# Sixty-four bytes behind each split-weight buffer of a hybrid decoder layer

## The chip, the core and the metric

The kernel runs on one core of one Trainium2 chip. The metric is the device time of one execution, in microseconds (us). The kernel before takes 1090.24 us, the median of three runs (1089.42, 1090.24 and 1090.95 us). The profile shown below is of another, single execution of the same program, which took 1090.18 us; its span from the first to the last recorded instruction is 1088.3 us, so 1.9 us lie around the span.

## What is computed

One decoder layer for 256 tokens of width 2048, in float32. Cut to the matrix products, which is where nearly all the time is:

```python
h = rmsnorm(x, pre_mix_g)
proj = h @ w_in                          # 2048 x 4368: q, k, v of two attention groups, forget gates
o_a = swa_sink_attention(...)            # 16 heads, window 128, sinks, ALiBi
o_b = forgetting_attention(...)          # 16 heads, learned forget gates
mix = concatenate([rmsnorm(o_a), rmsnorm(o_b)]) @ w_out      # 2048 x 2048
x = x + rmsnorm(mix, post_mix_g)
h = rmsnorm(x, pre_ffn_g)
u = causal_dwconv(h @ w_up, conv_w, conv_b)                  # 2048 x 11264
gate, val = split(u, 2)
y = (gelu(gate) * val) @ w_down                              # 5632 x 2048
x = x + rmsnorm(y, post_ffn_g)
```

All weights together are some 200 MB and each is used once, on 256 tokens.

## The kernel before

**Split operands.** Every float32 operand of a large product is kept as two tensors of the type float32r: a high part (the value as the copy to float32r leaves it) and a low part (the value less the high part). A product is then three matmuls: high by high, high by low and low by high.

**Weights.** `w_load` (L66) brings one unit of 128 x 1024 float32 (512 KB) by a DMA from SP's queue into one of five buffers named `raw`. `w_split` (L93) makes the two parts: ACT copies `raw` into a buffer `whi` (L103), and DVE subtracts `whi` from `raw` into a buffer `wlo` (L106). In one stage `w_high` (L81) does the same with L86 and L89. The buffers come from `w_parts` (L73). It has three cases: with `keep` unset, the ten ring buffers of the pool `wp`, five `whi` and five `wlo` (`WB = 5`, L64); with a pool in `keep`, buffers of that pool under the tags `hhi` and `hlo`; with `None` in `keep`, slices that the caller gives. The ring cases are nearly all: a `keep` with a pool is used for four units of the output projection, and the given slices for two units of the down projection. All these tensors are called `whi` and `wlo` in the profile, except the slices, which are called `rest`.

**Two ways in which PE reads the weights.** A matmul on this machine takes a stationary operand of 128 columns, which a weight load (PEld) brings in, and a moving operand that streams past it.

- In `unit_T` (L205) the weights are stationary. A unit has 8 slices of 128 columns (512 bytes in each partition) for each part. For each slice of `whi`, all 512 columns of `hT` (256 high, 256 low) stream past (L212); for each slice of `wlo`, the 256 high columns (L217). So a unit is 8 matmuls of 512 columns and 8 of 256. All of the q and k projections and the whole up projection go this way, the first four units of the up projection in a special form (L830, L834).
- In `mm3` (L241) the weights are moving. A stationary slice of 128 columns is taken from `hT` (the v projection), `oT` (the output projection) or `G` (the down projection), and a row of `whi` or `wlo` streams past it: L245, three matmuls for each pair, in the order `whi`, `wlo`, `whi`. The rows have 512 columns (2048 bytes) in the output and down projections. In the v projection they have 384 columns (1536 bytes), and in its last group 272 (1088 bytes). In that last group a unit holds three such rows one behind another, so they start 0, 1088 and 2176 bytes into the buffer, which is 0, 64 and 128 modulo 512. For each of the three rows, six matmuls follow one another.

**Order.** PE's instructions are in the order of the program (`manual_schedule`, L46). ACT, DVE, POOL and SP are placed by the framework's scheduler except in the stages where the program fixes them too.

**Addresses.** In SBUF each pool is laid out in the order `const`, `main`, `wp`, `small`, and then the pools of the stages. Three unused tiles named `room` (in `const`, `small` and `ffn`) shift what follows them. In the built program all large operands of PE start at a multiple of 512 bytes within a partition: `hT`, the five `raw`, the ten split buffers (from 106496 on, 4096 apart), `oT`, `G`, `keys`, `vpa` and `vpb`. Some tiles of the attention do not: `p`, `ph`, `pl`, `qh`, `ql` and `ident` start at 128 modulo 512.

- `L445` transposes a block of `p`: `p` is stationary at 128 modulo 512. `L681` transposes a block of `x_sb`: `x_sb` is stationary at 0. The moving operand of both is `ident`.
- `L454` and `L456` stream `ph` and `pl` (128 modulo 512, in two runs) past `vpa` or `vpb` (stationary, 0 modulo 512).

Of the kernel before, what the change touches and what calls it, by code (L numbers as in the profile page):

```python
# [8 lines left out]
F32 = mybir.dt.float32  # L9
F32R = mybir.dt.float32r  # L10
# [7 lines left out]
P = 128  # L18
# [12 lines left out]
def hybrid_layer(ctx: ExitStack, tc: tile.TileContext, x, pre_mix_g, w_in, b_forget, sinks,  # L31
# [10 lines left out]
    wp = ctx.enter_context(tc.tile_pool(name="wp", bufs=4))  # L42
    small = ctx.enter_context(tc.tile_pool(name="small", bufs=4))
# [19 lines left out]
    UNIT = 1024  # L63
    WB = 5  # L64
# [8 lines left out]
    def w_parts(n, keep=None):  # L73

        if keep and keep[0] is None:
            return keep[1]
        where, pre, nb = (keep[0], "h", keep[1]) if keep else (wp, "w", WB)
        return [where.tile([P, UNIT], F32R, tag=pre + x, bufs=nb, name="w" + x)[:, :n]
                for x in ("hi", "lo")]

    def w_high(unit, keep=None):  # L81

        raw, a, c = unit
        n = a * c
        hi, lo = w_parts(n, keep)
        act.copy(hi, raw[:, :n])  # L86

        def low():
            dve.tensor_tensor(lo, raw[:, :n], hi.bitcast(F32), op=ALU.subtract)  # L89

        return [x.rearrange("p (a c) -> p a c", a=a) for x in (hi, lo)], low

    def w_split(unit, pin=False, keep=None, begun=None, between=None):  # L93

        raw, a, c = unit
        n = a * c
        hi, lo = begun or w_parts(n, keep)
        for i in range(2 if between else 1):
            cs = slice(i * 512, i * 512 + 512) if between else slice(0, n)
            if i:  # L100
                between()
            if not between or i:
                i1 = act.copy(hi[:, cs], raw[:, cs])  # L103
                if pin:
                    tc.keep_in_program_order(i1)
            i2 = dve.tensor_tensor(lo[:, cs], raw[:, cs], hi[:, cs].bitcast(F32), op=ALU.subtract)  # L106
            if pin:
                tc.keep_in_program_order(i2)
        return [x.rearrange("p (a c) -> p a c", a=a) for x in (hi, lo)]

    def w_unit(src, a, c, keep=None):
        return w_split(w_load(src, a, c), keep=keep)

    def w_rows(w, k0, a, c0, c):
        return w[k0 * P:(k0 + a) * P, c0:c0 + c].rearrange("(a p) c -> p a c", p=P)
# [8 lines left out]


    const.tile([P, 120], F32, tag="room", name="room_c")
    small.tile([P, 368], F32, tag="room", bufs=1, name="room_s")

    gpre = const.tile([16, P], F32, tag="gpre", name="gpre")
    act.dma_start(gpre, pre_mix_g.rearrange("o (a p) -> (o a) p", p=P))  # L130
# [120 lines left out]
    with tc.tile_pool(name="mixp", bufs=1) as mp:  # L251
# [47 lines left out]


        begun = w_parts(UNIT)
        tc.keep_in_program_order(dve.tensor_copy(begun[0][:, 0:512], head[:, 0:512]))
        x_part(0, (0,), "acc")
# [246 lines left out]
        for p0, npair, cols in ((0, 3, 384), (3, 3, 384), (6, 2, 272)):  # L550
# [3 lines left out]
            for k0 in range(0, KT, per):  # L554
                na = min(per, KT - k0)
                hi, lo = w_unit(w_rows(w_in, k0, na, c0, cols), na, cols)
# [207 lines left out]
    with tc.tile_pool(name="ffn", bufs=1) as fp:  # L764
# [90 lines left out]
        for half in range(2):  # L855
# [42 lines left out]
            for n in range(3 + (half == 0)):  # L898
                b2 = [bank(), bank()]
                for u in range(FHALF // 2):  # L900
                    hi, lo = w_unit(w_rows(w_down, half * FHALF + u * 2, 2, n * 512, 512), 2, 512)
# [33 lines left out]
        for u in range(FHALF // 2):  # L935
            hi, lo = w_unit(w_rows(w_down, FHALF + u * 2, 2, 1536, 512), 2, 512,
                            keep=(None, [rest[:, c:c + 2, :].rearrange("p a c -> p (a c)")
                                         for c in (4 * (u - LAST), 4 * (u - LAST) + 2)])
                            if LAST <= u < FHALF // 2 - 4 else None)
# [56 lines left out]
```

## Time and profile before

| | |
|---|---|
| median of three runs | 1090.24 us |
| profiled execution, its own time | 1090.18 us |
| its span | 1088.3 us |
| mean granted TensorE clock | 0.996 |
| q, k, v projections and attention | 0 to 242 us |
| output projection, norms, residual | 242 to 342 us |
| up and down projection, first half | 342 to 713 us |
| up and down projection, second half | 713 to 1088 us |

In the profile an engine is busy while one of its instructions runs. Matmuls overlap: one that is listed with 389 ns starts some 227 ns after the one before. So the distance between the starts says what a matmul costs a full stream, and the listed length (which is longer by a nearly constant part) serves to compare matmuls of the same width. PEld is the weight load, which runs under the matmul before it. In the rows of the groups, the columns are: line, engine, operation, output <- inputs, shape and count | busy time in us, mean length of one in ns | idle time of the engine just before them, and what ended it. In the rows of a timeline, they are: start in us, length in us, engine, line, operation and count; neighbours of one kind are merged into a row.

### The profile page before, as it was taken

The page shows a single profiled execution, that of the slowest core. Times are in us where ns is not written, and L with a number is a line of the kernel's source. Part 1 is how long each engine was busy: PE and PEld are TensorE (multiplying, and loading weights), DVE is VectorE, ACT ScalarE, POOL GpSimd, SP SyncE. Part 2 cuts the span into 40 slices and gives each one's busy share as a digit, 9 for nine tenths or more (in the row PEclk, how much of TensorE's full clock was granted, in tenths as well). Part 3 has the DMA queues.
Part 4 walks back from the last instruction along what each step waited for, and adds up shares of the span by engine and source line. Part 5 has one row for each costly group of instructions (what it writes and reads, how often), then busy time and mean ns, then how long its engine had stood idle before and what let it go on. Part 6 is the DMA issues. An engine that isn't in the chain of part 4 may idle for free.

```text
span 1088.3 us, 16295 instructions
## 1 busy us (share of the span) xinstructions
PE 1075.0 (99%) x6002; PEld 932.2 (86%) x6002; DVE 739.7 (68%) x1193; ACT 625.7 (57%) x1069; POOL 183.3 (17%) x252
## 2 busy tenths in 40 slices
PE   9999999999999999999999999999999999999996
PEld 7889988887889888888888888888888888888886
DVE  5987877777567876776767544457777677765563
ACT  7766766666556765656656444456565565644450
POOL 3343344332022110101001000001010110101111
PEclk9999999999999999999999999999999999999998
DMA  8645565554872666656565666655665666666552
GB/s 291 196 129 170 174 190 177 153 158 152 284 243 104 213 197 193 191 178 198 186 193 183 199 192 194 197 189 180 189 195 182 192 191 186 184 196 192 193 171 78
DMA packets 164970, 202.88 MB, mean 186 GB/s; under 512 B 6780, under 2 KB 130972, under 8 KB 164380
## 3 DMA queue, kind: packets, MB, share of 16 engines
q1 hardware_dynamic: 164176, 201.27, 58.2%
q8 instruction: 47, 0.77, 0.3%
q10 hardware_dynamic: 716, 0.58, 0.2%
q14 instruction: 31, 0.25, 0.1%
HBM read 199.58 MB, written 2.11 MB: 185 GB/s over the span
## 4 chain that ended last, share of the span: by engine, by line
PE 89%; DVE 4%; ACT 3%; issue 1%; POOL 1%; DMA 1%; SPq 0%; DVEq 0%; POOLq 0%; ACTq 0%
PE bank_acc L245 34%; PE bank_acc L212 20%; PE bank_att L212 14%; PE bank_acc L217 10%; PE bank_att L217 7%; DVE wlo L106 2%; ACT whi L103 1%; POOL scr L377 1%; PE bank_att L410 1%; PE bank_att L454 1%; PE bank_att L445 1%; ACT p L428 1%; DMA x_in<-in_x_dram 1%; PE bank_att L456 0%; DVE hT L691 0%
## 5 line engine op out<-in xcount | busy, mean ns | idle before, releaser
L106 DVE TENSOR_TENSOR wlo<-raw,whi 128x1024 fp32r<-128x1024 f32 (+3 forms) x357 | 452.8, 1271 | 245.9 <-ACT whi L103 244.2
L103 ACT CAST whi<-raw 128x1024 fp32r<-128x1024 f32 (+3 forms) x356 | 368.5, 1037 | 235.9 <-PE bank_acc L245 119.0
L212 PE MATMUL bank_acc<-hT,whi 128*128 128x512 f32 x1120 | 286.7, 393 | 0.0
L212 PEld LDWEIGHTS bank_acc<-hT,whi 128*128 128x128 f32 x1120 | 200.0, 189 | 34.6
L245 PE MATMUL bank_acc<-whi,G 128*128 128x512 f32 (+1 forms) x724 | 214.8, 379 | 0.0
L212 PE MATMUL bank_att<-hT,whi 128*128 128x512 f32 x672 | 170.9, 392 | 0.1
L217 PEld LDWEIGHTS bank_acc<-hT,wlo 128*128 128x128 f32 x1120 | 151.3, 190 | 9.9
L217 PE MATMUL bank_acc<-hT,wlo 128*128 128x256 f32 x1120 | 157.6, 283 | 0.0
L245 PEld LDWEIGHTS bank_acc<-whi,G 128*128 128x128 f32 x724 | 133.8, 188 | 25.7 <-DVE y_sb L892 0.2
L801 POOL TENSOR_TENSOR u<-u,rowf 128x256 f32<-128x256 f32 x88 | 55.4, 651 | 543.3 <-DVE u L800 541.0
L212 PEld LDWEIGHTS bank_att<-hT,whi 128*128 128x128 f32 x672 | 120.7, 189 | 21.7 <-ACT whi L103 0.3
L245 PE MATMUL bank_acc<-wlo,G 128*128 128x512 f32 (+1 forms) x362 | 137.1, 379 | 0.0
L217 PEld LDWEIGHTS bank_att<-hT,wlo 128*128 128x128 f32 x672 | 91.7, 190 | 7.0 <-DVE wlo L106 0.4
L217 PE MATMUL bank_att<-hT,wlo 128*128 128x256 f32 x672 | 94.0, 282 | 0.0
L245 PE MATMUL bank_acc<-whi,oT 128*128 128x512 f32 (+1 forms) x272 | 83.1, 382 | 0.0
L245 PEld LDWEIGHTS bank_acc<-wlo,G 128*128 128x128 f32 x362 | 68.1, 188 | 12.8
L245 PEld LDWEIGHTS bank_acc<-whi,oT 128*128 128x128 f32 x272 | 50.4, 189 | 9.4
L245 PE MATMUL bank_acc<-wlo,oT 128*128 128x512 f32 (+1 forms) x136 | 51.5, 379 | 0.0
L245 PE MATMUL bank_acc<-whi,hT 128*128 128x384 f32 (+1 forms) x192 | 47.5, 323 | 0.0
L428 ACT ACTIVATE p<-p,nm 128x256 f32<-128x256 f32 (+1 forms) x64 | 28.4, 445 | 28.4 <-DVE nm L416 28.4
L377 POOL TENSOR_TENSOR scr<-scr 128x256 f32<-128x256 f32 x26 | 26.8, 1049 | 49.2 <-DVE scr L376 43.3
L799 ACT COPY cs<-bank_acc 128x256 f32<-128x256 f32 x48 | 15.9, 372 | 32.3 <-PE bank_acc L212 32.3
(187 smaller groups left out, 963.9 us busy)
## 6 DMA issues: line engine op xcount, KB each, us to landing
raw<-in_w_up_dram SPq DMA_DIRECT2D x176, 512.0 KB, 3.4
raw<-in_w_down_dram SPq DMA_DIRECT2D x88, 512.0 KB, 4.6
raw<-in_w_in_dram SPq DMA_DIRECT2D x51, 512.0 KB, 3.9
raw<-in_w_out_dram SPq DMA_DIRECT2D x32, 512.0 KB, 4.6
raw<-in_w_in_dram SPq DMA_DIRECT2D x16, 384.0 KB, 3.8
cb<-c_dram SPq DMA_DIRECT2D x8, 256.0 KB, 3.5
x_sb<-in_x_dram SPq DMA_DIRECT2D x2, 1024.0 KB
raw<-in_w_in_dram SPq DMA_DIRECT2D x5, 408.0 KB, 3.3
```

Source lines behind the costliest of these rows:

```text
L103: i1 = act.copy(hi[:, cs], raw[:, cs])
L106: i2 = dve.tensor_tensor(lo[:, cs], raw[:, cs], hi[:, cs].bitcast(F32), op=ALU.subtract)
L212: pe.matmul(b, hi[:, a, m * P:(m + 1) * P], hT[:, kt, :], start=(kt == 0), stop=(kt == KT - 1))
L217: pe.matmul(b[:, 256:512], lo[:, a, m * P:(m + 1) * P], hT[:, u * 4 + a, 0:256], start=False, stop=False)
L245: pe.matmul(b, a, r[:, cols], start=(first and i == 0), stop=(last and i == 2))
L377: pool.tensor_tensor(dst, dst, row, op=ALU.mult)
L410: pe.matmul(sb[e][:, cs], a[r, t * P:(t + 1) * P], b[r, 0:nk], start=(n == 0), stop=(n == 2))
L428: act.activation(p[:, e, cs], p[:, e, cs], AF.Exp, bias=nm[:, t, e:e + 1], scale=-1.0, accum_out=rs[:, t, e:e + 1])
L445: pe.transpose(pb[:, i * P:(i + 1) * P], p[:, e, c:c + P], ident)
L454: pe.matmul(ov, values(hl, 0), p[:, :, 0:256], start=(n == 0), stop=False)
L799: act.copy(c, b[:, 256:512])
L801: pool.tensor_tensor(u[:, 2:258], u[:, 2:258], rowf, op=ALU.mult)
```

## The change

`w_parts` gives the ring buffers of the pool `wp` 1040 columns in place of 1024 and goes on using the first 1024; the cases with `keep` are as before. The unused tile in `small` shrinks from 368 to 208 columns, by 640 bytes, which is ten times 64.

```diff
         if keep and keep[0] is None:
             return keep[1]
-        where, pre, nb = (keep[0], "h", keep[1]) if keep else (wp, "w", WB)
-        return [where.tile([P, UNIT], F32R, tag=pre + x, bufs=nb, name="w" + x)[:, :n]
+        if keep:
+            return [keep[0].tile([P, UNIT], F32R, tag="h" + x, bufs=keep[1], name="w" + x)[:, :n]
+                    for x in ("hi", "lo")]
+
+        return [wp.tile([P, UNIT + 16], F32R, tag="w" + x, bufs=WB, name="w" + x)[:, :n]
                 for x in ("hi", "lo")]
...
     const.tile([P, 120], F32, tag="room", name="room_c")
-    small.tile([P, 368], F32, tag="room", bufs=1, name="room_s")
+    small.tile([P, 208], F32, tag="room", bufs=1, name="room_s")
```

In the built program the five `whi` then start at 0, 64, 128, 192 and 256 modulo 512, and the five `wlo` at 320, 384, 448, 0 and 64. Every other tensor keeps its address. Each engine has the same instructions with the same shapes and waits in the same order; only the addresses of the ten buffers in them differ. All lines after the edited function move down by 3.

## The prediction

> **What bounds the kernel now.** I read the page first, then the groups with their shapes kept apart, then the chain of waits, and last a timeline of a stage in which the weights already lie off 512.
>
> ```profile
> span 1088.3 us, 16295 instructions
> ...
> PE 1075.0 (99%) x6002; PEld 932.2 (86%) x6002; DVE 739.7 (68%) x1193; ACT 625.7 (57%) x1069; POOL 183.3 (17%) x252
> ...
> PE 89%; DVE 4%; ACT 3%; issue 1%; POOL 1%; DMA 1%; SPq 0%; DVEq 0%; POOLq 0%; ACTq 0%
> PE bank_acc L245 34%; PE bank_acc L212 20%; PE bank_att L212 14%; PE bank_acc L217 10%; PE bank_att L217 7%; DVE wlo L106 2%; ACT whi L103 1%; POOL scr L377 1%; PE bank_att L410 1%; PE bank_att L454 1%; PE bank_att L445 1%; ACT p L428 1%; DMA x_in<-in_x_dram 1%; PE bank_att L456 0%; DVE hT L691 0%
> ```
>
> PE is busy for 99% of the span and makes 89% of the chain that ended last. The three lines that read the changed buffers, L245, L212 and L217, hold 34 + 20 + 14 + 10 + 7 = 85% of it. So the time moves with the distance between the starts of these matmuls, and with hardly anything else. The weight loads show the counts, and whether PE waits for the split:
>
> ```profile
> L212 PEld LDWEIGHTS bank_acc<-hT,whi 128*128 128x128 f32 x1120 | 200.0, 189 | 34.6
> L217 PEld LDWEIGHTS bank_acc<-hT,wlo 128*128 128x128 f32 x1120 | 151.3, 190 | 9.9
> L245 PEld LDWEIGHTS bank_acc<-whi,G 128*128 128x128 f32 x724 | 133.8, 188 | 25.7 <-DVE y_sb L892 0.2
> L212 PEld LDWEIGHTS bank_att<-hT,whi 128*128 128x128 f32 x672 | 120.7, 189 | 21.7 <-ACT whi L103 0.3
> L217 PEld LDWEIGHTS bank_att<-hT,wlo 128*128 128x128 f32 x672 | 91.7, 190 | 7.0 <-DVE wlo L106 0.4
> L245 PEld LDWEIGHTS bank_acc<-wlo,G 128*128 128x128 f32 x362 | 68.1, 188 | 12.8
> L245 PEld LDWEIGHTS bank_acc<-whi,oT 128*128 128x128 f32 x272 | 50.4, 189 | 9.4
> L245 PEld LDWEIGHTS bank_acc<-whi,hT 128*128 128x128 f32 x192 | 33.6, 188 | 0.3
> L245 PEld LDWEIGHTS bank_acc<-wlo,oT 128*128 128x128 f32 x136 | 25.9, 190 | 4.4
> L245 PEld LDWEIGHTS bank_acc<-wlo,hT 128*128 128x128 f32 x96 | 18.1, 188 | 0.0
> ```
>
> The listed waits for `whi` and `wlo` are 0.3 and 0.4 us. The weights are moving in 724 + 362 + 272 + 136 + 192 + 96 = 1782 matmuls, and stationary in 1120 + 672 = 1792 of 512 columns (L212) and 1792 of 256 (L217): 5366 in all.
>
> **The change, part by part.** It removes and adds no instruction, DMA or wait, and moves none past another. What is new is where eight of the ten ring buffers lie (two stay at 0 modulo 512). The five engines' work on them has these costs.
>
> *The DMAs* write `raw`, which stays in its place: nothing.
>
> *The split on ACT and DVE.*
>
> ```profile
> L106 DVE TENSOR_TENSOR wlo<-raw,whi 128x1024 fp32r<-128x1024 f32 (+3 forms) x357 | 452.8, 1271 | 245.9 <-ACT whi L103 244.2
> L103 ACT CAST whi<-raw 128x1024 fp32r<-128x1024 f32 (+3 forms) x356 | 368.5, 1037 | 235.9 <-PE bank_acc L245 119.0
> ```
>
> Nearest rows for another address, both casts by ACT in SBUF, the first into a tile at 0 and the second into one at 128 modulo 512:
>
> ```profile
> L248 ACT CAST G<-yv 128x256 fp32r<-128x256 f32 x44 | 16.3, 407 | 23.0 <-DVE yv L878 23.0
> ...
> L248 ACT CAST qh<-scr 128x256 fp32r<-128x256 f32 x16 | 6.4, 410 | 11.5 <-POOL scr L377 11.3
> ```
>
> That is 3 ns in 407, under 1%. ACT waits 235.9 us in total before L103, most of it for PE to release a buffer, and DVE 245.9 us before L106, for ACT. So what either loses or gains lies under PE's matmuls: cost nothing. Without that cover, in the first 30 us, L106 and L103 are themselves on the chain with 2% and 1% of the span, 33 us; 1% of this is 0.3 us, and it is in the range, not in the sum.
>
> *Weights as the moving operand (L245).* What a matmul costs now is read from the longest piece of the chain:
>
> ```profile
> 593.38 119.69 PE bank_acc L245 x528
> ```
>
> 119.69 / 528 = 226.7 ns for 512 columns, without a hole. For a moving row off 512 the profile has a direct case: the last group of the v projection, whose three rows lie at 0, 64 and 128 modulo 512 in the same buffer, six matmuls each. The timeline of PE, with one row in each six kept (the first with `wlo`):
>
> ```profile
> 115.62 0.29 PE L245 MATMUL bank_acc<-wlo,hT 128*128 128x272 f32 x1
> ...
> 116.38 0.29 PE L245 MATMUL bank_acc<-wlo,hT 128*128 128x272 f32 x1
> ...
> 117.13 0.29 PE L245 MATMUL bank_acc<-wlo,hT 128*128 128x272 f32 x1
> ...
> 117.89 0.28 PE L245 MATMUL bank_acc<-wlo,hT 128*128 128x272 f32 x1
> ...
> 118.63 0.29 PE L245 MATMUL bank_acc<-wlo,hT 128*128 128x272 f32 x1
> ...
> 119.38 0.29 PE L245 MATMUL bank_acc<-wlo,hT 128*128 128x272 f32 x1
> ```
>
> ```profile
> 125.90 0.29 PE L245 MATMUL bank_acc<-wlo,hT 128*128 128x272 f32 x1
> ...
> 126.66 0.29 PE L245 MATMUL bank_acc<-wlo,hT 128*128 128x272 f32 x1
> ...
> 127.41 0.28 PE L245 MATMUL bank_acc<-wlo,hT 128*128 128x272 f32 x1
> ...
> 128.15 0.29 PE L245 MATMUL bank_acc<-wlo,hT 128*128 128x272 f32 x1
> ...
> 128.91 0.29 PE L245 MATMUL bank_acc<-wlo,hT 128*128 128x272 f32 x1
> ...
> 129.67 0.28 PE L245 MATMUL bank_acc<-wlo,hT 128*128 128x272 f32 x1
> ```
>
> The first stretch begins at a row with offset 0, the second at one with offset 64. So the sixes at 0 take 0.76, 0.74 and 0.74 us, 124.4 ns for one matmul; those at 64 take 0.75, 0.75, 0.76 and 0.76, 125.8 ns; those at 128 take 0.76, 0.75 and 0.76, 126.1 ns. Off 512 a matmul is later by about 1.5 ns. Each start is rounded to 10 ns, so anything from 0 to 3 ns fits.
>
> *Weights as the stationary operand (L212, L217).* When nothing but the load sets the pace, its address does not show:
>
> ```profile
> L445 PEld LDWEIGHTS bank_att<-ident,p 128*128 128x128 f32 x96 | 11.4, 140 | 1.5
> ...
> L681 PEld LDWEIGHTS bank_att<-ident,x_sb 128*128 128x128 f32 x32 | 3.6, 140 | 0.1
> ```
>
> `p` lies at 128 modulo 512 and `x_sb` at 0, and both loads take 140 ns. But under a stream of 256 or 512 columns two reads run together, and what the change alters is how far apart they start. In the v projection, too, one of the two starts off the other by 64 or 128. I take that price here as well, 1.5 ns, since those rows have both reads going and the transposes do not; its lower end is 0.
>
> *The farther bounds* are the only matmuls whose two operands both are apart for another reason, `ph` and `pl` (128) past `vpa` (0):
>
> ```profile
> L212 PE MATMUL bank_acc<-hT,whi 128*128 128x512 f32 x1120 | 286.7, 393 | 0.0
> L245 PE MATMUL bank_acc<-whi,G 128*128 128x512 f32 x652 | 202.8, 389 | 0.0
> ...
> L217 PE MATMUL bank_acc<-hT,wlo 128*128 128x256 f32 x1120 | 157.6, 283 | 0.0
> ...
> L454 PE MATMUL bank_att<-ph,vpa 128*128 128x512 f32 x16 | 5.0, 393 | 0.0
> ...
> L454 PE MATMUL bank_att<-pl,vpa 128*128 128x512 f32 x8 | 3.2, 398 | 0.0
> L456 PE MATMUL bank_att<-ph,vpa 128*128 128x256 f32 x16 | 3.2, 279 | 0.0
> ```
>
> At 512 columns they are up to 398 - 389 = 9 ns longer, at 256 columns 283 - 279 = 4 ns shorter. They stream in two runs, so they are farther from the changed matmuls than the 272-column rows are. Price per matmul: 1.5 ns taken, -4 and +9 kept for the range.
>
> *The sum.* 0.8 of 5366 matmuls are 4293; by 1.5 ns, 6.4 us. On the profiled execution's 1090.18 us that is 1096.6, and on the median, 0.06 us higher, 1096.7 us: slower by 0.6%.
>
> **The rivals.**
>
> *The address does not matter to PE: no change.* For it speak the two equal loads of 140 ns, and that 0 ns still fits the rounding of the 272-column rows. Against it, that the sixes at 64 and 128 come out longer in both stretches. It would give 1090.2 us. The Trainium skill, page "SBUF — State Buffer", section "Who interferes with whom", says the same: PE has two independent read ports, one for the moving operand and one for the weight load, and never waits on anyone. By that rule the sum would be 0; the equal loads agree, the 272-column rows lean against it.
>
> *Spreading the buffers ends a collision: faster.* Before, the weight load and the stream of the matmul above it start at the same place modulo 512 in each of the 5366 matmuls. If both then ask for the same part of the memory, each pays for it, and moving one by 64 or more frees them. L456, with its operands 128 apart, is 4 ns shorter than L217. If only the 1792 matmuls of L217 gain that on 0.8 of them, it is 5.7 us: 1084.5 us. If all 5366 do, 17.2 us: 1073.1 us. Against it: the 272-column rows at 64 and 128 had the same chance and were not shorter. It decides from the point at which the relief is larger than the 1.5 ns.
>
> *A slice that runs over a boundary of 512 costs more than the 272-column rows show: clearly slower.* A stationary slice of 512 bytes fits one stretch of 512 before and lies in two after; a moving row of 2048 lies in four before and in five after. The 272-column row of 1088 bytes lies in three at each of its offsets, so it cannot show that price. L454, at 9 ns, can. On 0.8 of the 1792 matmuls of L212 and the 724 + 362 + 272 + 136 = 1494 of L245 (a few of them are narrower) it is 0.8 x 3286 x 9 = 23.7 us: 1113.9 us. Against it: L456 runs over one boundary more in each of its runs, and is short.
>
> **How the numbers follow.** Mild slowing 0.46; boundary price 0.14; no change 0.16; faster 0.24. The forecast is 1096.7 us. Its own range goes from 1.5 ns on the 1782 moving matmuls alone (0.8 x 1782 x 1.5 = 2.1 us, 1092.4) to 3 ns on all (12.9 us, 1103.1). The range for 8 in 10 takes in the boundary price, and of the faster case what 2.8 ns on all matmuls would bring (12 us): 1078 to 1114 us. Out of it are the larger gains, about 0.08, and the larger losses, about 0.08. About 0.2% (2.2 us) is what a measurement of this kernel can tell from no change: faster 0.24, within 0.16, slower 0.60.
>
> **What would show it.** The chain's long piece of L245 in the down projection would go from 226.7 ns to about 228 ns a matmul, and L212 and L217 would lengthen from 393 and 283 ns by one or two. PE would stay at 99% and the waits for `whi` and `wlo` under 1 us. If only L245 moves, the stationary price is 0. If L217 shortens, the collision was real. If lengths rise by 5 ns or more, it is the boundary. I am wrong in kind if PE's rows do not move but its idle time does, for then ACT or DVE has become the limit.

## The result, and the profile after

The changed kernel takes 1094.5 us, the median of six runs (1093.78 to 1095.34), against 1089.83 us for the kernel before in six runs (1089.26 to 1091.17). The ratio is 1.0045, with a 95% interval of 1.0035 to 1.0056: slower by 0.45%, or 4.67 us. The profiled execution of it took 1094.73 us.

From the page of the changed kernel, its span, the busy time of the engines, the chain's shares by engine, and the groups that answer to those shown of before (L248, L215, L220, L109 and L106 are the former L245, L212, L217, L106 and L103):

```profile
span 1092.9 us, 16295 instructions
...
PE 1079.7 (99%) x6002; PEld 928.6 (85%) x6002; DVE 740.4 (68%) x1193; ACT 624.7 (57%) x1069; POOL 185.6 (17%) x252
...
PE 92%; DVE 3%; ACT 2%; issue 1%; POOL 1%; DMA 1%; SPq 0%; DVEq 0%; POOLq 0%; ACTq 0%
...
L109 DVE TENSOR_TENSOR wlo<-raw,whi 128x1024 fp32r<-128x1024 f32 (+3 forms) x357 | 453.2, 1272 | 247.6 <-ACT whi L106 247.3
L106 ACT CAST whi<-raw 128x1024 fp32r<-128x1024 f32 (+3 forms) x356 | 367.7, 1035 | 237.2 <-PE bank_acc L248 128.0
...
L215 PEld LDWEIGHTS bank_acc<-hT,whi 128*128 128x128 f32 x1120 | 199.1, 188 | 35.3
```

PE is still busy for 99% of the span, and its 4.7 us more (1075.0 to 1079.7) are the whole difference of the spans, 4.6 us. The split takes what it took: 1272 ns against 1271 on DVE, 1035 against 1037 on ACT. The weight loads are listed with 188 ns (189 before). So PE waits for nothing longer; its matmuls themselves stand farther apart. Which ones, the groups with their shapes kept apart tell (busy us, mean ns of one | idle us). After:

```profile
L215 PE MATMUL bank_acc<-hT,whi 128*128 128x512 f32 x1120 | 288.1, 394 | 0.0
L248 PE MATMUL bank_acc<-whi,G 128*128 128x512 f32 x652 | 205.7, 394 | 0.0
...
L220 PE MATMUL bank_acc<-hT,wlo 128*128 128x256 f32 x1120 | 155.5, 281 | 0.0
L248 PE MATMUL bank_acc<-wlo,G 128*128 128x512 f32 x326 | 128.3, 393 | 0.0
```

And one row of before that the prediction did not show:

```profile
L245 PE MATMUL bank_acc<-wlo,G 128*128 128x512 f32 x326 | 126.9, 389 | 0.0
```

In the down projection, where the weights move, a matmul is listed 4 to 5 ns longer (394 and 393 against 389 and 389). Where they are stationary, the one of 512 columns is 1 ns longer (393 to 394) and the one of 256 is 2 ns *shorter* (283 to 281).

The chain of waits in order of time gives the same in microseconds (start us, length us, what). Before, the three long pieces:

```profile
285.58 49.13 PE bank_acc L245 x216
593.38 119.69 PE bank_acc L245 x528
958.88 120.87 PE bank_acc L245 x594
```

After:

```profile
285.30 50.09 PE bank_acc L248 x216
593.65 122.36 PE bank_acc L248 x528
961.45 122.85 PE bank_acc L248 x594
```

The piece at 285 us is in the output projection: 0.96 us longer, 4.4 ns for each of 216. The piece at 593 us is the first half of the down projection: 2.67 us longer, from 226.7 to 122.36 / 528 = 231.7 ns for a matmul, 5.0 ns more. The last piece, the second half, is 1.98 us longer. Between the two halves lies the second half of the up projection, 88 units (11264 / 2 columns in blocks of 256, four units each), from the end of the one piece to the start of the other: 958.88 - 713.07 = 245.81 us before and 961.45 - 716.01 = 245.44 us after, 2793 and 2789 ns for a unit. It gained 4 ns a unit.

Of the 4.6 us of the span, 2.67 + 1.98 are the down projection, -0.37 the second half of the up projection, and 0.27 all that comes before 593 us. That last one is too small by about 1.8 us, for the profiled execution of before had a slower clock within a stretch of 20 us, and that of after had not. The view by stretches (stretch us, its length, then busy us of PE, PEld, DVE, ACT and POOL with counts, granted clock, DMA share, GB/s), before and then after:

```profile
240.00:260.00 20.00, 18.68 (x91) 15.20 (x90) 15.49 (x33) 13.28 (x30) 6.46 (x9) 0.91 0.42 137
```

```profile
240.00:260.00 20.00, 18.73 (x99) 15.19 (x98) 15.18 (x34) 13.26 (x31) 6.47 (x9) 1.00 0.47 141
```

At a clock of 0.91, about 0.09 x 20 = 1.8 us are lost, an estimate. So at equal clocks the first 593 us lost some 2 us, of which the output projection's piece is one.

### The profile page after: what moved, and what is told of

It reads as the page before. It is cut to its first block, busy times and chain, and to the rows that moved or that the text cites. A ratio compares the mean times of both kernels' runs of the same rounds, so it can differ in the third digit from the quotient of the medians.

```text
span 1092.9 us, 16295 instructions
## 1 busy us (share of the span) xinstructions
PE 1079.7 (99%) x6002; PEld 928.6 (85%) x6002; DVE 740.4 (68%) x1193; ACT 624.7 (57%) x1069; POOL 185.6 (17%) x252
## 4 chain that ended last, share of the span: by engine, by line
PE 92%; DVE 3%; ACT 2%; issue 1%; POOL 1%; DMA 1%; SPq 0%; DVEq 0%; POOLq 0%; ACTq 0%
PE bank_acc L248 34%; PE bank_acc L215 21%; PE bank_att L215 14%; PE bank_acc L220 11%; PE bank_att L220 7%; DVE wlo L109 2%; PE bank_att L413 1%; PE bank_att L457 1%; PE bank_att L448 1%; ACT whi L106 1%; POOL scr L380 1%; PE bank_att L459 0%; DMA x_in<-in_x_dram 0%; DVE hT L694 0%; ACT p L431 0%
## 5 line engine op out<-in xcount | busy, mean ns | idle before, releaser
L109 DVE TENSOR_TENSOR wlo<-raw,whi 128x1024 fp32r<-128x1024 f32 (+3 forms) x357 | 453.2, 1272 | 247.6 <-ACT whi L106 247.3
L106 ACT CAST whi<-raw 128x1024 fp32r<-128x1024 f32 (+3 forms) x356 | 367.7, 1035 | 237.2 <-PE bank_acc L248 128.0
L215 PE MATMUL bank_acc<-hT,whi 128*128 128x512 f32 x1120 | 288.1, 394 | 0.0
L215 PEld LDWEIGHTS bank_acc<-hT,whi 128*128 128x128 f32 x1120 | 199.1, 188 | 35.3
L248 PE MATMUL bank_acc<-whi,G 128*128 128x512 f32 (+1 forms) x724 | 217.6, 382 | 0.0
L215 PE MATMUL bank_att<-hT,whi 128*128 128x512 f32 x672 | 172.7, 395 | 0.0
L220 PEld LDWEIGHTS bank_acc<-hT,wlo 128*128 128x128 f32 x1120 | 149.7, 188 | 10.9
L248 PEld LDWEIGHTS bank_acc<-whi,G 128*128 128x128 f32 x724 | 133.7, 188 | 29.0 <-DVE y_sb L895 0.2
L220 PE MATMUL bank_acc<-hT,wlo 128*128 128x256 f32 x1120 | 155.5, 281 | 0.0
L215 PEld LDWEIGHTS bank_att<-hT,whi 128*128 128x128 f32 x672 | 120.8, 189 | 22.0
L248 PE MATMUL bank_acc<-wlo,G 128*128 128x512 f32 (+1 forms) x362 | 138.4, 382 | 0.0
L220 PEld LDWEIGHTS bank_att<-hT,wlo 128*128 128x128 f32 x672 | 91.2, 189 | 7.5
L220 PE MATMUL bank_att<-hT,wlo 128*128 128x256 f32 x672 | 92.9, 280 | 0.0
L248 PE MATMUL bank_acc<-whi,oT 128*128 128x512 f32 (+1 forms) x272 | 83.4, 383 | 0.0
L248 PEld LDWEIGHTS bank_acc<-wlo,G 128*128 128x128 f32 x362 | 68.0, 188 | 14.2
L248 PEld LDWEIGHTS bank_acc<-whi,oT 128*128 128x128 f32 x272 | 50.2, 188 | 10.3
L248 PE MATMUL bank_acc<-wlo,oT 128*128 128x512 f32 (+1 forms) x136 | 51.7, 380 | 0.0
L248 PE MATMUL bank_acc<-whi,hT 128*128 128x384 f32 (+1 forms) x192 | 47.7, 325 | 0.0
```

The lines of the kernel that those rows point to most:

```text
L215: pe.matmul(b, hi[:, a, m * P:(m + 1) * P], hT[:, kt, :], start=(kt == 0), stop=(kt == KT - 1))
L220: pe.matmul(b[:, 256:512], lo[:, a, m * P:(m + 1) * P], hT[:, u * 4 + a, 0:256], start=False, stop=False)
L248: pe.matmul(b, a, r[:, cols], start=(first and i == 0), stop=(last and i == 2))
```

## The experiments

Four theories stood after the result. *Boundary:* an operand that runs over a multiple of 512 bytes is slower, wherever the other one lies. *Distance:* what counts is how far apart, modulo some period, the moving row and the stationary slice start (in the profile the weight load runs under a matmul, so both are read at the same time). *Mixture:* what counts is that the ten buffers differ from one another. *None:* PE does not see addresses, and something else made the difference. In all kernels below but the two scans, every engine has the same instructions with the same shapes and waits in the same order as before; only addresses differ. What each kernel moves is told against the kernel before, and each ratio is against that kernel on the same chip. (The edits of `w_parts` are made in the changed kernel's text: the lines shown replace its ring case.)

Two numbers are read from each run's chain: the first down piece by 528 (ns for a matmul with moving weights of 512 columns), and the stretch from its end to the start of the next long piece by 88 (ns for an up unit of 8 matmuls of 512 and 8 of 256 columns). Before they are 226.7 and 2793. "Distance" is the offset of the split buffer less that of `hT` (or of `G`, which stays at 0 in every kernel but the first), in bytes. After the experiments, a table gathers them.

### All operands moved together

```diff
-    const.tile([P, 120], F32, tag="room", name="room_c")
+    const.tile([P, 136], F32, tag="room", name="room_c")
```

Everything from `x_in` on, so all large operands of PE, lies 64 bytes farther. Each slice and row of before now runs over one boundary of 512 more, and all distances stay 0.

> Everything from x_in on lies 64 bytes higher: raw, the ten split buffers, hT, oT, G, keys, vpa and vpb all start at 64 modulo 512, so each operand runs over one boundary of 512 more, but no two operands of a matmul are moved against each other. Boundary theory (a slice or row costs more when it does not itself start at 512): slower than the changed kernel, since all ten buffers and the other operands are off, 1089.8 + 4.7 x 10/8 = 1095.7 us or more. Distance theory (what counts is how far apart, modulo 512, the moving operand and the weight load beside it start): no change, 1089.8 us within 1.5. Mixture theory (what counts is that the ten buffers differ from one another): no change as well.

```profile
593.11 119.69 PE bank_acc L245 x528
958.60 120.66 PE bank_acc L245 x594
```

1089.48 us against 1089.69, ratio 1.0000 (0.9990 to 1.0009). Both numbers are those of before, 226.7 and 2793 ns (245.80 / 88). A boundary of 512 costs nothing here, and the place by itself does not matter. The boundary theory falls.

### The ring alone moved by 64

All ten buffers at 64, everything else in place. This edit of `w_parts` is shared by the ring kernels below; they differ in the numbers in its tuple (columns of 4 bytes) and in `room_s`, which takes up the difference.

```diff
+        out = []
+        for x, ahead, pad in (("hi", 16, 0), ("lo", 0, 0)):
+            if ahead and x not in shifted:
+                shifted.append(x)
+                wp.tile([P, ahead], F32, tag="room" + x, bufs=1, name="room_" + x)
+            out.append(wp.tile([P, UNIT + pad], F32R, tag="w" + x, bufs=WB, name="w" + x)[:, :n])
+        return out
```

> All ten split buffers at 64 modulo 512, hT, oT and G at 0. Mixture theory: the buffers are alike, so no change, 1089.8 us within 1.5. Boundary theory: ten buffers off in place of eight, 1089.8 + 4.7 x 10/8 = 1095.7 us. Distance theory: every pair is 64 apart; from the rows of the changed kernel for its buffers at 64, the up projection's unit hardly moves (+12 ns for L212, -10 for L217) and a moving row is some 4 ns later, 1490 x 4 = 6 us: 1095 to 1096 us, and L245 in the down projection at about 231 ns a matmul.

```profile
591.02 120.87 PE bank_acc L253 x528
955.94 121.12 PE bank_acc L253 x594
```

1088.34 us, ratio 0.9984 (0.9975 to 0.9994): faster, which none of the theories had said. The down projection went to 228.9 ns, as a distance should show, though by 2 ns and not by the 4 expected. But an up unit, which was hardly to move, fell from 2793 to 2773 ns (244.05 / 88). So one distance is a loss in the down projection, whose matmuls in this piece have 512 columns, and a gain in the up unit, where half of them have 256. Whether the use or the width decides, the groups tell further down.

### Buffers spread by 512, and by 256

First the five `whi` 512 bytes farther apart than before, which moves the `wlo` and all that follows by whole steps of 512, so that everything stays at 0 modulo 512; then 256 unused bytes behind each of the ten buffers, which lie at 0 and 256 in turn:

```diff
+        for x, ahead, pad in (("hi", 0, 128), ("lo", 0, 0)):
```

> The five whi are 4608 apart in place of 4096, the wlo move up by 2560, and what follows by 1536: all still start at 0 modulo 512, but at different places modulo 4096. All three theories as they stand, with 512 as the period: no change, 1089.8 us within 1.5. If the period is longer than 512, the split buffers now lie differently against hT and G and the time moves as in the changed kernel, by 3 us or more.

```diff
+        for x, ahead, pad in (("hi", 0, 64), ("lo", 0, 64)):
```

> The change with 256 unused bytes behind each of the ten buffers in place of 64: they lie at 0, 256, 0, 256, 0 and 256, 0, 256, 0, 256 modulo 512, all at 0 modulo 256. If the period is 256, as the first look's equal blocks at 0 and 256, 64 and 320, 128 and 384, 192 and 448 say: no change, 1089.6 us within 1.5, and 226.7 ns a matmul in the down projection. If the period is 512: half of the pairs are 256 apart, and the time moves as in the changed kernel, by 3 us or more.

The first took 1090.39 us, ratio 1.0007 (0.9997 to 1.0016); the second 1090.09 against 1089.85 us, 1.0001 (0.9992 to 1.0011). The chain of the second:

```profile
595.24 119.69 PE bank_acc L253 x528
960.73 78.91 PE bank_acc L253 x348
```

226.7 and 2793 ns (245.80 / 88), with half of the buffers at 256. That the buffers lie at different places is not what costs, so the mixture theory falls, and a distance of 256 is as good as 0: the period is 256, not 512. (The second down piece is cut in two in this chain, so its length is not compared.)

### The other operand moved

If it is the distance, then moving `hT` must do in the up projection what moving the ring did there, and nothing in the down projection, where the stationary slice is from `G`. `hT` at 448 makes the distance 64, as in the kernel with the ring at 64; `hT` at 64 makes it 448, which is 192 modulo 256.

```diff
+    main.tile([P, 112], F32, tag="room_a", name="room_a")
...
+    main.tile([P, 16], F32, tag="room_b", name="room_b")
```

> The kernel before with hT alone 448 bytes higher (64 unused bytes behind it); ring, oT and G stay at 0 modulo 512. So in the q, k and up projections the stationary weights lie 64 above the moving hT, as with all buffers at 64, and in the output and down projections the distance is 0, as before. Distance theory: the up projection as with the ring at 64 (L212 at 232.7 and L217 at 114.0 ns from start to start, 21 ns less a unit, 224 units: 4.7 us less), the down projection as before (226.7 ns): 1085.0 us, faster than both kernels. If the absolute place of the weights counted after all: 1089.7 us, the up projection unmoved.

```profile
590.43 119.70 PE bank_acc L247 x528
954.19 120.64 PE bank_acc L247 x594
```

1085.0 us against 1089.55, ratio 0.9959 (0.9944 to 0.9974). The up unit is at 2773 ns (244.06 / 88), that of the ring at 64; the down projection is at 226.7. The kernel has 224 units with stationary weights (1792 / 8): 224 x 20 ns = 4.5 us, and 4.55 us were gained. The groups show where in a unit:

```profile
L214 PE MATMUL bank_acc<-hT,whi 128*128 128x512 f32 x1120 | 289.5, 396 | 0.0
...
L219 PE MATMUL bank_acc<-hT,wlo 128*128 128x256 f32 x1120 | 152.5, 278 | 0.0
```

The 512 columns are 3 ns longer than before (396 against 393), the 256 columns 5 ns shorter (278 against 283); eight of each make -16 ns of the 20.

Is it the use or the width? In the last column block of the down projection, where the weights move, there are rows of 256 columns too. Before:

```profile
L245 PE MATMUL bank_acc<-whi,G 128*128 128x256 f32 x72 | 15.0, 283 | 0.0
```

With the ring at 64, so that `G` and `whi` are 64 apart:

```profile
L253 PE MATMUL bank_acc<-whi,G 128*128 128x512 f32 x652 | 204.0, 391 | 0.0
...
L253 PE MATMUL bank_acc<-whi,G 128*128 128x256 f32 x72 | 14.4, 277 | 0.0
```

With `hT` at 448, which leaves this distance at 0, the narrow rows stand at 282. So at a distance of 64 the wide matmuls are longer and the narrow ones shorter in both uses: by 2 and 6 ns where the weights move, by 3 and 5 where they are stationary. The sign goes with the width here, not with the use.

The same with 16 columns ahead of `hT` and 112 behind:

> The kernel before with hT alone 64 bytes higher, so that the stationary weights lie 448, which is 192 modulo 256, above the moving hT; the distance in the output and down projections stays 0. Distance theory with the paces of the first look: the up projection's unit alternates between 2735 and 2778 ns, 2757 on average, 36 ns less than before; 224 units: 8.1 us less, 1081.5 us. If it is the size of the shift and not its sign that counts, 64 bytes up is as 64 down: 1085.0 us.

```profile
590.12 119.73 PE bank_acc L247 x528
952.45 120.75 PE bank_acc L247 x594
```

1082.84 us against 1089.85, ratio 0.9929 (0.9913 to 0.9946). The up unit is at 2757 ns (242.60 / 88). The timeline of PE in the second half of the up projection (start us, length us) shows that it is a mean of two:

```profile
800.24 2.00 PE L214 MATMUL bank_acc<-hT,whi 128*128 128x512 f32 x8
802.07 1.07 PE L219 MATMUL bank_acc<-hT,wlo 128*128 128x256 f32 x8
802.98 1.99 PE L214 MATMUL bank_acc<-hT,whi 128*128 128x512 f32 x8
804.80 1.11 PE L219 MATMUL bank_acc<-hT,wlo 128*128 128x256 f32 x8
805.75 2.00 PE L214 MATMUL bank_acc<-hT,whi 128*128 128x512 f32 x8
```

From 800.24 to 802.98 is 2.74 us, from 802.98 to 805.75 is 2.77: in one unit the eight of 256 columns take 0.91 us (802.07 to 802.98), in the next 0.95 (804.80 to 805.75), at the same distance and in turn.

This pair is also the plainest case against the theory that PE does not see addresses. The Trainium skill, page "SBUF — State Buffer", section "Who interferes with whom", gives PE two independent read ports and says that PE never waits on anyone. By that rule all these kernels would have taken the time of before, and the ratio of 0.9929 says that here they do not.

### A map of the distances

Two kernels with rings of four (`WB = 4`, tiles of `UNIT + 128` columns) set the offsets of `whi` and `wlo` anew for each block of the up projection (eight units) and for each column block of the down projection. Each was executed once (1096.21 and 1098.62 us). Their own time tells nothing, since the block changes mix distances; the blocks at 0 have the paces of the kernel before.

```diff
+        return [wp.tile([P, UNIT + 128], F32R, tag="w" + x, bufs=WB, name="w" + x)[:, at[x]:at[x] + n]
...
+                start(*UP[half][g])
...
+                start(*DOWN[half][n])
```

> One look at many distances in one program. The split buffers are 4608 apart and a unit starts at a chosen place in its buffer, with one choice for each block of eight units of the up projection and for each column block of the down projection; rings of four, to have the room. Distance theory: each block has its own steady pace, repeated to a nanosecond in its units; with both kinds at 0 the unit takes 2793 ns as before, with both at 64 some 2772, with whi at 256 and wlo at 320 some 2780 (not among them: whi at 256, wlo at 64); in the down projection 226.7 ns a matmul at 0, 228.9 at 64, some 232 at 256. If the pace were a matter of the buffers being alike, all blocks would take the same. The whole time tells nothing here, since the blocks differ.

> The second look at distances, with the same program and other choices: steps of 16 bytes, and the two kinds at different distances. Distance theory: again one steady pace for each block, equal to a nanosecond or alternating between units, between 2735 and 2823 ns a unit; at 192 in the down projection the same as the 233 ns found at 448, if the period is 256. The theory gives no number for the new distances; the blocks are there to find out whether a shorter unit than 2735 ns, or a shorter matmul than 226.7 ns in the down projection, exists.

From PE's timeline in the first of them, rows of `whi` six units apart in the blocks at 64, 192 and 256, and two units apart at 320:

```profile
419.95 2.02 PE L218 MATMUL bank_att<-hT,whi 128*128 128x512 f32 x8
...
436.59 2.02 PE L218 MATMUL bank_att<-hT,whi 128*128 128x512 f32 x8
...
487.13 2.00 PE L218 MATMUL bank_acc<-hT,whi 128*128 128x512 f32 x8
...
503.67 2.00 PE L218 MATMUL bank_acc<-hT,whi 128*128 128x512 f32 x8
...
509.20 2.00 PE L218 MATMUL bank_att<-hT,whi 128*128 128x512 f32 x8
...
525.96 2.00 PE L218 MATMUL bank_att<-hT,whi 128*128 128x512 f32 x8
...
531.53 2.02 PE L218 MATMUL bank_acc<-hT,whi 128*128 128x512 f32 x8
...
537.08 2.02 PE L218 MATMUL bank_acc<-hT,whi 128*128 128x512 f32 x8
```

At 64: 16.64 / 6 = 2773 ns. At 192: 16.54 / 6 = 2757. At 256: 16.76 / 6 = 2793. At 320: 5.55 / 2 = 2775, that of 64. The other blocks were read in the same way, from the units behind the first of a block, and the down projection's as the mean distance of the starts in a column block. The table has a part of them; the means of the others lie between 2773 and 2827 ns and between 232 and 233.3:

| both parts at a distance of | up unit, ns | down matmul, ns |
|---|---|---|
| 0, 256 | 2793 | 226.7 |
| 16 | 2760 | 231.7 |
| 32 | 2813 | 233.3 |
| 48 | 2814 | 233.3 |
| 64, 320 | 2773 | 228.9 |
| 128 | 2805 to 2815 | 232.4 |
| 160 | 2827 | 234.3 |
| 192, 448 | 2735 and 2778 in turn | 233.3 |
| 208 | 2793 | 230 |
| `whi` 192, `wlo` 64 | 2747 | not tried |

In the down projection no distance tried was as good as 0. In the up projection 0 is in the middle of the field: 192 with 64 is 46 ns better, 160 is 34 ns worse. Two expectations missed: the down projection at 256 was to take some 232 ns and takes 226.7, and 2827 lies above the 2823 given as the upper end for a unit.

The width is not all. With `hT` at 64, a distance of 192, the up projection's matmuls of 512 columns start 228.9 ns apart on average, 1.2 less than before; the down projection's lose 6.6 ns at 192. There the use, or the order in which wide and narrow matmuls follow one another, counts as well, and no run separates these two.

### One half of the change at a time

`whi` spread as in the change with all `wlo` at 0, then `wlo` spread with all `whi` at 0:

```diff
+        for x, ahead, pad in (("hi", 0, 16), ("lo", 48, 0)):
```

> Half of the change: the five whi at 0, 64, 128, 192 and 256 as in the changed kernel, all five wlo back at 0. If the parts add up as the changed kernel's rows stand (L212 +1.5 ns on 1792, moving whi +5 ns on two thirds of 1490): 7.7 us more, 1097.4 us, slower than the whole change, whose wlo then gave 3 us back. If only the distance of each matmul's own pair counted, the wlo matmuls would be as before (119.1 and 226.7 ns); if the pace carries over from one matmul to the next, they move too.

```diff
+        for x, ahead, pad in (("hi", 0, 0), ("lo", 80, 16)):
```

> The other half: all whi at 0, the five wlo at 320, 384, 448, 0 and 64 as in the changed kernel. If the parts add up (L217 -2.0 ns on 1792, moving wlo +5 ns on a third of 1490): 3.6 us less and 2.5 us more, 1088.6 us, no change within 0.2%. If the pace carries over, whi's matmuls move as well, though whi lies where it lay.

The first took 1094.92 us, ratio 1.0049 (1.0033 to 1.0065), the second 1092.9 us, 1.0029 (1.0017 to 1.0042), both against 1089.55. The halves cost 5.4 and 3.4 us, 8.7 together, and the whole change 4.67: they do not add up, and both times lie off those expected from adding (1097.4 and 1088.6). The groups say why. With `whi` alone spread:

```profile
L253 PE MATMUL bank_acc<-whi,G 128*128 128x512 f32 x652 | 204.8, 392 | 0.0
...
L253 PE MATMUL bank_acc<-wlo,G 128*128 128x512 f32 x326 | 128.1, 393 | 0.0
```

With `wlo` alone spread:

```profile
L253 PE MATMUL bank_acc<-whi,G 128*128 128x512 f32 x652 | 204.3, 391 | 0.0
...
L253 PE MATMUL bank_acc<-wlo,G 128*128 128x512 f32 x326 | 128.1, 393 | 0.0
```

In the first the `wlo` lie where they lay, and still take 393 ns in place of 389; in the second the `whi` do, and take 391. In a stream of `whi`, `wlo`, `whi` a matmul is slowed by the distance of its neighbours. It is so from one unit to the next as well. Take the first half of the down projection in the first kernel (starts from its trace, sorted by the addresses of the buffers). A unit there is twelve matmuls. The units with `whi` at 256 come behind those at 0 and take 226.7 ns at each of their twelve places. The units at 0 come behind those at 128: at their first eight places they take 228 to 235 ns, and 226.7 only at the last four.

### Two parts at distances of their own, a first try

All `whi` at 256 and all `wlo` at 320, to keep the down projection's `whi` at a distance of 0 and have the up projection's gain of 64 on the `wlo`:

```diff
+        for x, ahead, pad in (("hi", 64, 0), ("lo", 16, 0)):
```

> All five whi at 256 modulo 512, all five wlo at 320, everything else in its place. Distance theory: the changed kernel's one whi buffer at 256 and one wlo buffer at 320 were its shortest in the up projection, 10 and 48 ns a unit under the kernel before; with all buffers there, 224 units x 58 ns = 13 us less, and 1490 moving rows by 5 ns, 7.5 us more: about 1084.3 us, with L217 at 113 ns from start to start. Boundary theory: as with any other offset, 1095.7 us. Mixture theory: within a kind the buffers are alike, so no change, 1089.8 us, or slightly slower since the two kinds differ.

```profile
592.04 122.50 PE bank_acc L253 x528
959.18 122.87 PE bank_acc L253 x594
```

1093.12 us, ratio 1.0038 (1.0023 to 1.0053): a miss of the distance theory as it stood then. The up unit is at 2780 ns (244.64 / 88), 13 below before where all buffers at 64 brought 20, and the down projection is at 232.0 ns, above that with all at 64 (228.9) though two of three rows are at 0. Mixed distances are a case of their own: this and the halves are the same finding.

### Each use at its own distance

`hT` at 64 as above, so that the down projection keeps 0, and `wlo` 128 bytes into its buffer in the units that are read as stationary: distances of 192 for `whi` and 64 for `wlo`, the best pair of the map.

```diff
+        at = 32 if c == 256 else 0
+        return [hi, wp.tile([P, UNIT + 64], F32R, tag="wlo", bufs=WB, name="wlo")[:, at:at + n]]
...
+    main.tile([P, 16], F32, tag="room_a", name="room_a")
...
+    main.tile([P, 112], F32, tag="room_b", name="room_b")
```

> hT 64 bytes higher as in the run before, and where the weights are stationary (q, k and up projections) wlo starts 128 bytes into its buffer, which has 256 more; where they are moving it starts at 0. So whi lies 192 and wlo 64 above hT modulo 256, the pair whose unit settled at 2747 ns in the second look, and the output and down projections keep distance 0. If a pace carries over from that look: 46 ns a unit less than before, 224 units, 10.3 us: 1079.5 us, and a steady 2747 ns in the up projection. If the settling there was a matter of what stood ahead of it (its first units took 2781, 2807 and 2761 ns), somewhere between 1079 and 1090 us. In any case the down projection stays at 226.7 ns a matmul.

The chain, and then PE's timeline in the second half of the up projection:

```profile
587.62 119.73 PE bank_acc L250 x528
949.07 120.75 PE bank_acc L250 x594
```

```profile
802.88 2.00 PE L217 MATMUL bank_acc<-hT,whi 128*128 128x512 f32 x8
804.71 1.07 PE L222 MATMUL bank_acc<-hT,wlo 128*128 128x256 f32 x8
805.62 2.00 PE L217 MATMUL bank_acc<-hT,whi 128*128 128x512 f32 x8
...
813.86 2.00 PE L217 MATMUL bank_acc<-hT,whi 128*128 128x512 f32 x8
```

1080.22 us (1080.03 to 1081.89) against 1089.27, ratio 0.9922 (0.9905 to 0.9938): 0.8% faster than the kernel before and, by the two ratios (0.9922 / 1.0045), 1.2% faster than the changed one, by addresses alone. The up unit is at 2747 ns (241.72 / 88), every one of them now with the eight narrow matmuls in 0.91 us (804.71 to 805.62).

### All of them together

| kernel | distances | up unit, ns | down matmul, ns | ratio |
|---|---|---|---|---|
| before | 0 | 2793 | 226.7 | |
| the change | 0 to 448, by 64 | 2789 | 231.7 | 1.0045 |
| all operands moved by 64 | 0 | 2793 | 226.7 | 1.0000 |
| `whi` 512 farther apart | 0 | 2793 | 226.7 | 1.0007 |
| buffers at 0 and 256 in turn | 0, 256 | 2793 | 226.7 | 1.0001 |
| ring at 64 | 64 | 2773 | 228.9 | 0.9984 |
| `hT` at 448 | up 64, down 0 | 2773 | 226.7 | 0.9959 |
| `hT` at 64 | up 192, down 0 | 2757 | 226.8 | 0.9929 |
| `whi` spread, `wlo` at 0 | 0 to 256, by 64, and 0 | 2799 | 230.4 | 1.0049 |
| `whi` at 0, `wlo` spread | 0, and 320 to 64, by 64 | 2790 | 229.9 | 1.0029 |
| `whi` 256, `wlo` 320 | 0 and 64 | 2780 | 232.0 | 1.0038 |
| `hT` at 64, `wlo` by use | up 192 and 64, down 0 | 2747 | 226.8 | 0.9922 |

## Why the prediction was right in sign and size, and wrong in its parts

*The forecast* was slower by 0.6%, 1096.7 us; it is slower by 0.45%, 1094.5 us. That PE's starts set the time held, and so did the cover of the split: PE stayed at 99%, and ACT's and DVE's durations stood within 2 ns.

*The moving operand* is the term that was mis-sized: 1.5 ns on 0.8 of the matmuls is 1.2 ns on each, and the down projection's piece shows 5.0, the output projection's 4.4. The term was to be 2.1 us (0.8 x 1782 x 1.5); 978 matmuls by 5.0 and 360 by 4.4 ns are 6.5 us, an estimate. The rows of 272 columns that gave the price were read rightly: by the starts in the trace they stand 124.6 ns apart at a distance of 0 and 126.0 at 128. But they were no fit measure, for three reasons that the runs show. The price depends on the width: at 128, rows of 512 columns lose 5.7 ns in the map, and at 192, where those lose 6.6, the rows of 272 even gain (123.7 ns, in the kernel with `hT` at 64). Their distances were 0, 64 and 128, while those of the changed kernel, modulo 256, are these and 192. And the price holds for a stream at one distance; the change gave neighbouring matmuls different ones, and then also those at 0 pay (in the experiment with one half of it, 393 ns for a `wlo` left at 0). In the changed kernel, too, the starts in the down projection sorted by buffer put the first `whi`, which stayed at 0, at 232 ns or more against 226.7.

*The stationary operand* was the wrong step: "I take that price here as well, 1.5 ns". It was to cost 16 x 0.8 x 1.5 = 19 ns a unit, and the unit became 4 ns shorter. The eight 512-column matmuls lost 1.5 ns each (the mean distance of their starts in the up projection went from 230.1 to 231.6) and the eight 256-column ones gained 2.0 (119.1 to 117.1): together -4 ns. One price could not serve all widths: at 64, matmuls of 256 columns are shorter and those of 512 longer, whether the weights move or not. The prediction's own rows had these signs, L454 up to 9 ns longer at 512 columns and L456 4 ns shorter at 256, but it used them for the range and the rivals and not for the sum. This term was to be 4.3 us (0.8 x 3584 x 1.5) and was some -0.9 us (224 units by -4 ns, an estimate).

That the total came out near the forecast is luck: the two errors, a moving term some four times too small and a stationary term of the wrong sign, were of opposite direction.

*The collision.* The mark set for it was "If L217 shortens, the collision was real". L217 did shorten, by 2 ns, and the experiments with `hT` show that a distance of 0 costs the up projection up to 46 ns a unit against the best one found. So of the narrow matmuls that rival had the direction right at some distances, but not its reason: at 160, where the two start farther apart than at 64, the unit is 34 ns longer than at 0. It lost because the down projection has its best at 0, and because the change spread the buffers over good and bad distances alike. A version that keeps 0 where it is best and leaves it where it is not is faster than both.

*The boundary.* The mark for it, lengths up by 5 ns or more, was met by the rows of `whi` in the down projection (389 to 394). It is nonetheless wrong: with all operands off 512 by 64 nothing changed. That mark could not tell a boundary from a distance; only moving both operands together could.

*No change at all* falls with `hT` at 448 and at 64, where the same instructions took 0.4% and 0.7% less.

What stays open: why a distance costs what it does. The runs show that the time depends on the distance modulo 256 bytes; which part of PE's reading, or of the memory, this belongs to, no run here separates. In the up projection the ring and `hT` were each moved alone, with the same 2773 ns; in the down projection `G` was never moved alone, so that it is the distance from `G` that counts there, and not from another tensor that stayed, is carried over and not shown. Nor is it shown why units at a distance of 192 take 2.74 and 2.77 us in turn.

## What to carry to other kernels

Where PE is the limit and every matmul brings a weight load, the places of the moving and the stationary operand relative to one another are worth a trial: here they alone moved the kernel between 1080.2 and 1094.9 us. Set them for each use apart, since the best distance for one shape and order is not that of another, and give all buffers of a ring the same distance rather than spreading them. To tell an effect of the place from one of the distance, move both operands together once, and then each alone.

## What was not expected of the hardware

- The period is 256 bytes: with buffers at 0 and 256 in turn the ratio is 1.0001, and the blocks at 64 and 320 of the map have 2773 and 2775 ns, alike to the rounding of the rows.
- The best distance has no common rule: down matmuls of 512 columns take 226.7 ns at 0 and 256 and 228.9 to 234.3 elsewhere, while up units take 2747 ns at 192 and 64, 2793 at 0, and 2827 at 160.
- The sign depends on the width: at 64, matmuls of 512 columns are listed 2 to 3 ns longer and those of 256 columns 5 to 6 ns shorter, in both uses.
- The pace carries over: a matmul whose own operands did not move becomes 2 to 4 ns longer when its neighbours' distances change, and a unit at 0 behind one at 128 needs eight matmuls to come back to 226.7 ns.
- The listed length of a load says nothing of it: 188 ns in the changed kernel, 189 before, in a kernel that is 4.67 us longer. The matmuls' starts and lengths show it.
